# One inference step of a hybrid streaming encoder on one core: the next head's key parts moved beside the scores, memory heads written from PSUM into the projection's operand, open tiles filled chunk by chunk

## Chip, cores and metric

One core of a Trainium2 chip runs the whole step as one program. The metric is the device time of the execution in microseconds (us), the median of several runs; the profile is one execution taken by the hardware profiler.

## What is computed

Two token groups go through a trunk of two layers at once: 1024 new tokens of a stream (the prompt) and 32 tokens of a running stream (the decode group), model width 1024, all in fp32. Layer 0 mixes tokens by causal pooling, layer 1 by differential attention; both attend, with 4 heads of 128 channels, to 256 memory tokens. Cut to what matters here:

```
h = rmsnorm(x, g_attn[l]);  z = h @ w_in[l];  mix, qm = split(z)
m_out = mem_attend(qm, mem_k[l], mem_v[l])                     # 4 memory heads
layer 0:  t_out = pool_mix(mix)                                # 4 groups of 128 channels
layer 1:  k, v = split(rmsnorm(x, g_kv) @ w_kv)                # 4 heads, keys [K1 | K2] of 64 channels each
          for c in (1, 2):  p[c] = softmax(q[c] @ k[c].T / 8 + alibi, chunk-causal)
          t_out = rmsnorm((p[1] - lam * p[2]) @ v, g_subln) * (1 - lam_init)
x = x + concat(t_out, m_out) @ w_out[l]                        # the output projection
x = x + relu(rmsnorm(x, g_ffn[l]) @ w_ff1[l])**2 @ w_ff2[l]
```

Outputs are the final rmsnorm for both groups, the memory keys and values, the new keys and values, and pooling states.

## The kernel before

Activations are kept transposed, 128 channels by tokens: 8 chunks of channels, and the 1056 tokens (1024 + 32) in three groups of 352, the decode tokens at the end of group 2. Each fp32 product is made of three fp32r matmuls: every operand is split into a high part (a cast on ScalarE) and a low part (a subtraction on VectorE or GpSimd; `split`, line 54), and `mm3` (line 47) issues high × high, high × low, low × high. `g_dense` (line 142) makes one output tile of 128 channels by 352 tokens from 8 chunks, 24 matmuls. Weights come by DMA on SP's queue into raw tiles (tag `wraw`, six of them, line 86) and are split ahead of their use (`part`, `weight_split`, `weight`, lines 99 to 132). The operand of the projections is `xh[g]`, `xl[g]` per token group (line 175).

The program is traced in an order written by hand, and a tile scheduler then fixes each engine's order at compile time; each engine runs its own order strictly. The hand-written order is a main stream (a generator of attention work) beside a filler (a generator of projections): `drive` and `step` (lines 476 to 512) advance the main stream by one piece, then at most one piece of the first job in `queue`, then one piece of each job in `side`, and then spend filler matmuls worth `ratio` times the time those pieces say they take. `until(key)` (line 466) yields None until `key` is in `self.done`, which ends the filler's turn; `need` (line 531) runs the filler until something exists.

Layer 1 (`mix1`, line 917): the main stream is `diff_unit` (line 900), four diff-attention heads of four query pairs each (a pair is 256 queries; pair n looks at 256 (n + 1) keys), then `mem_unit` (line 451), four memory heads in two halves of 512 queries. The filler `fill1` (line 938) makes, head by head, the projections of keys, values and queries (`diff_project`, line 679), then the four memory queries (`mem_project`, line 335), then begins the output projection (`open_tiles`, line 953). `diff_project` evicts the keys' three groups into `kst` (line 686, one buffer), the values into `vst` (line 696) and the queries into `qf` (line 705), splits these into `Q` on ScalarE and GpSimd and copies halves of it by DMA. Before the scores of a head, `diff_unit` waits for its projections (`need`), then makes the key parts KS (`diff_keys`, line 729: eight casts of 64 × 256 on ScalarE, lines 736 and 737, and eight subtractions on VectorE, lines 738 and 739; one buffer), rescales the distance table `dtab` (line 906) and goes through the pairs. `diff_scores` (line 767) makes scores (784, 785), adds the table and finds the minimum on VectorE (791), takes the exponential on ScalarE (793), and combines the two maps (764, 765). `diff_values` (808) comes three rounds later: transposes (826), a split of them into `aTh` and `aTl` (55, 56), products with V.

A memory head (`mem_load_kv`, `mem_scores`, `mem_values`, lines 355 to 413): scores, softmax, transposes, split into `aTh`, `aTl`, values in a PSUM tile `po`. Heads 0 to 2 are copied to `mo` on ScalarE (405) and stored to `oscr` in HBM (406); head 3 is split from PSUM into chunk 7 of the operand (413). `mem_sample` (415) does the same for the 32 decode rows of the four heads. `new_x` (948) allocates the operand for the output projection once the last memory query projection is issued. `head` (973) loads a chunk's three token groups from `oscr` into raw tiles and splits them into `xh`, `xl`. `open_tiles` loads chunks 0 to 6 and makes six output tiles from them, two in `dn` banks and four in `sc` banks once the last scores are done; `project` (1013) adds chunk 7 to these six, adds x, and makes the other tiles. The loads of x for this (990, 992) are issued at the start of `tail` (980).

Of the kernel before, what the change touches and what calls it, by code (L numbers as in the profile page):

```python
# [9 lines left out]
F32 = mybir.dt.float32  # L10
F32R = mybir.dt.float32r
# [5 lines left out]
SEQ = 1024  # L17
NS = 32
NT = SEQ + NS
GW = 352  # L20
NG = 3
C = 8
# [8 lines left out]
NRAW = 6  # L31
NWB = 14
WARM = 9
STEPS = 44
LAG = 22
T2_AT, T_AT = 8, 20
ORDER = (2, 0, 1)
YOFF = 896
# [3 lines left out]
class Kern:  # L42
# [188 lines left out]

    def setup(self):
        nc, t, ctx, tc = self.nc, self.t, self.ctx, self.tc
        self.done = set()
        self.pu, self.pend, self.last_exp, self.last_add = {}, [], None, None
        self.wlist, self.wraw, self.wready, self.ahead, self.wstop = self.weights(), [], [], 1, False
        self.base = ctx.enter_context(tc.tile_pool(name="base", bufs=1))
        self.dram = ctx.enter_context(tc.tile_pool(name="dram", bufs=1, space=bass.MemoryType.DRAM))
        self.wpool = ctx.enter_context(tc.tile_pool(name="wpool", bufs=1))
        self.wplace = None  # L240
        self.xpool = ctx.enter_context(tc.tile_pool(name="xpool", bufs=1))
        self.xh, self.xl, self.rs = [None] * NG, [None] * NG, [None] * NG
        b = self.base
        self.gains = b.tile([128, 69], F32, name="gains")
        self.ones = b.tile([128, 128], F32, name="ones")
        nc.vector.memset(self.ones, 1.0)
        self.epsc = b.tile([128, 1], F32, name="epsc")
        nc.vector.memset(self.epsc, EPS)
        self.kscr = [[self.dram.tile([128, 256], F32, name=f"kscr{l}{h}") for h in range(4)] for l in range(2)]
        self.vscr = [[self.dram.tile([128, 2, 128], F32, name=f"vscr{l}{h}") for h in range(4)] for l in range(2)]  # L250
        self.oscr = [[self.dram.tile([128, NT], F32, name=f"oscr{l}{c}") for c in range(8)] for l in range(2)]
        self.xscr = [self.dram.tile([128, C, GW], F32, name=f"xscr{g}") for g in range(NG)]
# [132 lines left out]
    def mem_values(self, l, h, half, p, kv, pr):  # L385
        nc = self.nc
        v = kv[1]
        parts = []
        for a in range(2):
            pt = self.mmtile()  # L390
            for i in range(4):
                b = 256 * i + 128 * a
                nc.tensor.transpose(pt[:, 128 * i:128 * i + 128], pr[:, b:b + 128], self.ident)
            ph = p.tile([128, 512], F32R, tag="aTh", name="aTh", bufs=2)
            pl = p.tile([128, 512], F32R, tag="aTl", name="aTl", bufs=2)
            self.split(ph, pl, pt)
            parts.append((ph, pl))
            yield 0.6
        po = self.mmtile()
        for a in range(2):  # L400
            self.mm3(po, v[:, 0, a], v[:, 1, a], parts[a][0], parts[a][1], a == 0, a == 1)
            yield 0.65
        if h < 3:
            o = p.tile([128, 512], F32, tag="os", name="mo", bufs=2)
            nc.scalar.copy(o, po)
            nc.sync.dma_start(self.oscr[l][4 + h][:, 512 * half:512 * half + 512], o)
            self.done.add(("o", l, h, half))
            return
        for g in range(NG):
            a, b = max(512 * half, g * GW), min(512 * half + 512, (g + 1) * GW)  # L410
            if a < b:
                s = slice(a - g * GW, b - g * GW)
                self.split(self.xh[g][:, C - 1, s], self.xl[g][:, C - 1, s], po[:, a - 512 * half:b - 512 * half])

    def mem_sample(self, l, p, qs):

        nc, t = self.nc, self.t
# [18 lines left out]
        po = self.mmtile()[:, :128]  # L436
        for h in range(4):
            for a in range(2):
                b = 128 * a + NS * h
                nc.tensor.matmul(po[:, NS * h:NS * h + NS], lhsT=vc[:, h, a, :], rhs=aT[:, b:b + NS],  # L440
                                 start=a == 0, stop=a == 1)
        o = p.tile([128, 4, NS], F32, tag="os", name="oss", bufs=2)
        nc.scalar.copy(o.rearrange("p a b -> p (a b)"), po)
        for h in range(3):
            nc.sync.dma_start(self.oscr[l][4 + h][:, SEQ:], o[:, h, :])
        s = slice(GW - NS, GW)
        self.split(self.xh[2][:, C - 1, s], self.xl[2][:, C - 1, s], o[:, 3, :])
        self.done.add(("o", l, "s"))
        yield 0.6

# [228 lines left out]
    def diff_project(self, h, p, out, smp):  # L679
        nc, t = self.nc, self.t  # L680
        W = self.weight()
        kst = self.pd.tile([128, NT], F32, tag="kst", name="kst", bufs=1)
        for g in ORDER if h == 0 else range(NG):
            ps = self.dntile()[:, :GW]
            yield from self.g_dense(ps, W, g)
            nc.vector.tensor_tensor(kst[:, g * GW:(g + 1) * GW], ps, self.rs[g], ALU.mult)
        nc.sync.dma_start(t["kT"][h], kst)

        W = self.weight()
        if h:  # L690
# [2 lines left out]
        for g in range(NG):  # L693
            ps = self.dntile()[:, :GW]
# [6 lines left out]
        for g in range(NG):  # L701
# [22 lines left out]
                        nc.sync.dma_start(qd[o, c], qd[b, c])  # L724
            if g == NG - 1:
                nc.gpsimd.tensor_copy(smp["q"][:, h, :], qf[:, GW - NS:])
        out[h] = {"vst": vst, "kst": kst, "Q": Q}

    def diff_keys(self, h, d, p, smp):
        nc = self.nc  # L730
        kst = d["kst"]
        KS = self.pd.tile([128, 2, SEQ], F32R, tag="ks", name="KS", bufs=1)
        KSf = KS.bitcast(F32)
        for a in range(4):
            s = slice(256 * a, 256 * a + 256)
            nc.scalar.copy(KS[0:64, 0, s], kst[0:64, s])
            nc.scalar.copy(KS[64:128, 1, s], kst[64:128, s])
            nc.vector.tensor_tensor(KS[64:128, 0, s], kst[0:64, s], KSf[0:64, 0, s], ALU.subtract)
            nc.vector.tensor_tensor(KS[0:64, 1, s], kst[64:128, s], KSf[64:128, 1, s], ALU.subtract)
        d["KS"] = KS  # L740
        nc.gpsimd.tensor_copy(smp["k"][:, h, :], kst[:, SEQ:])

    def diff_vals(self, h, d, p, smp):
        nc = self.nc
# [22 lines left out]
    def diff_scores(self, h, pair, p, d, A):  # L767
        nc = self.nc
        Wk = 256 * (pair + 1)
        q = d["Q"][pair]  # L770
        KS = d["KS"]
        for i in (2 * pair, 2 * pair + 1):
            qc = slice((i % 2) * 128, (i % 2) * 128 + 128)
            Wi = max(256, 128 * (i + 1))
# [75 lines left out]
    def diff_sample(self, p, smp):  # L850

        nc, t = self.nc, self.t
        sc = self.sctile()
        kv = self.pd.tile([128, 2, 4, 256], F32, tag="ks", name="kvc", bufs=1)
        kc, vc = kv[:, 0], kv[:, 1].rearrange("p h (a e) -> p h a e", a=2)
        nc.scalar.dma_start(kc, t["ck"])
        nc.scalar.dma_start(vc, t["cv"])
# [42 lines left out]
    def diff_unit(self, p, fill, dd, smp):  # L900
        for h in range(4):
            self.need(fill, dd, h)
            d = dd[h]
            self.diff_keys(h, d, p, smp)
            r = 8.0 * SLOPES[0] if h == 0 else SLOPES[h] / SLOPES[h - 1]
            self.nc.vector.tensor_scalar(self.dtab, self.dtab, r, None, ALU.mult)
            if h:
                yield from self.wait(2)
            self.later(0, self.diff_vals(h, d, p, smp))
            for pair in range(4):  # L910
                A = []
                yield from self.backlog(2)
                yield from self.diff_scores(h, pair, p, d, A)
                self.later(3, self.diff_values(h, pair, p, d, A))
        self.side.append(self.diff_sample(p, smp))

    def mix1(self):
        self.nq, self.nmk = 4, 1
        with self.tc.tile_pool(name="attd", bufs=1, reuse_waits="tile") as self.pd, \
                self.tc.tile_pool(name="att1", bufs=1, reuse_waits="tile") as p:  # L920
            dd, qq = {}, {}
            self.qp = p
            self.claim(self.pd, (("kst", NT, 1), ("vst", NT, 1), ("ks", 2 * SEQ, 1), ("v", 2 * SEQ, 1), ("pA2", 768, 2),
                                 ("std", 8, 4), ("pad", 672, 1)))
            self.claim(p, (("q", 1024, self.nq), ("qf", GW, 2), ("st", 16, 4), ("pA3", 1024, 2), ("aTh", 512, 2),
                           ("aTl", 512, 2), ("mkr", 256, 1), ("mk", 512, 1), ("pad", 128, 1)))
# [26 lines left out]
    def open_tiles(self, l):  # L953

        W = self.W = {}
        self.open = []
        for c in range(C - 1):
            if c > 3:
                for key in (("o", l, c - 4, 0), ("o", l, c - 4, 1), ("o", l, "s")):
                    yield from self.until(key)  # L960
            self.head(l, c)
            if c < 3:
                W[c] = self.weight()
        places = [(0, 0), (0, 1), (0, 2), (1, 0), (1, 1), (1, 2)]
        for n, (g, j) in enumerate(places):
            if n == 2:
                yield from self.until(("m", l, 3, 1))
                X = [t[:, 512 * i:512 * i + 512] for t in (self.sctile(), self.sctile()) for i in range(2)]
            ps = (self.dntile() if n < 2 else X[n - 2])[:, :GW]
            self.open.append((g, j, ps))  # L970
            yield from self.g_dense(ps, W[j], g, range(C - 1))

    def head(self, l, c):

        for g in range(NG):
            o = self.wpool.tile([128, 512], F32, tag="wraw", name="o", bufs=NRAW)[:, :GW]
            self.nc.sync.dma_start(o, self.oscr[l][c][:, g * GW:(g + 1) * GW])
            self.take(o, g, c, pool=())

    def tail(self, l):  # L980
        nc, t = self.nc, self.t
# [658 lines left out]
```

## Time and profile before

| what | us |
|---|---|
| runs: 2127.57, 2129.15, 2131.08; median | 2129.15 |
| the profiled execution's own time | 2129.38 |
| its span, first to last instruction | 2127.6 |
| TensorE (PE) busy | 2093.3 |
| VectorE (DVE) busy | 1686.8 |
| ScalarE (ACT) busy | 1129.7 |
| GpSimd (POOL) busy | 568.3 |

The mean granted TensorE clock is 0.994 of full speed (1 is 2.4 GHz, 0.5 is 1.2 GHz). Times in the rows are us from the start of the span. PE's busy time counts pipelined matmuls with modelled ends. In a row of the trace, "out<-in" names the tile written and those read, and brackets at the end give the idle time of the engine just before and what released it. Layer 0's attention stage runs from about 30 to 225, its feed-forward part to about 960, layer 1's diff attention from about 980 to 1250, its memory heads to 1340, and the rest is layer 1's output projection and feed-forward part.

### The profile page before, as it was taken

What the parts mean: (1) busy time and instruction counts of PE and PEld (TensorE: products, weight loads), DVE (VectorE), ACT (ScalarE), POOL (GpSimd) and SP (SyncE); (2) the same over time, 40 slices, a digit from 0 to 9 for tenths busy, and PEclk for the clock granted to TensorE, in tenths of its full rate; (3) what the DMA queues carried; (4) which work ended last, traced back from release to release, by engine and by line L of the source; (5) the groups of instructions that cost most, each with busy time, mean ns of one, the idle gap of its engine ahead of it and who ended that gap; (6) DMA issues with size and microseconds to landing.
All of it is one profiled execution on the core that took longest, in us unless ns stands there. A gap on an engine that the chain in (4) does not pass through costs nothing. (4 is left out here: it accounts for less than half of the span.)

```text
span 2127.6 us, 35390 instructions
## 1 busy us (share of the span) xinstructions
PE 2093.3 (98%) x13068; PEld 2052.6 (96%) x13068; DVE 1686.8 (79%) x3160; ACT 1129.7 (53%) x2437; POOL 568.3 (27%) x577
## 2 busy tenths in 40 slices
PE   9999999999999999999999999999999999999997
PEld 8999999999999999999998897999999999999997
DVE  8856498888888888867777876489888888888865
ACT  7546364444444444455766766355444444444454
POOL 1021113343334333320111112104333333333323
PEclk9999999999999999999999999999999999999999
DMA  5635321111111111124222114511111111111112
GB/s 194 191 110 184 124 60 56 45 55 45 56 45 55 45 55 45 56 82 154 66 72 74 45 38 134 176 50 50 45 55 45 55 45 55 44 57 45 56 40 82
DMA packets 89997, 159.01 MB, mean 75 GB/s; under 512 B 13280, under 2 KB 32096, under 8 KB 89312
## 3 DMA queue, kind: packets, MB, share of 16 engines
q1 hardware_dynamic: 87952, 151.78, 22.5%
q10 hardware_dynamic: 1872, 4.98, 0.7%
q8 instruction: 102, 1.67, 0.3%
q14 instruction: 71, 0.58, 0.1%
HBM read 127.72 MB, written 24.80 MB: 72 GB/s over the span
## 5 line engine op out<-in xcount | busy, mean ns | idle before, releaser
L50 PE MATMUL dn<-xh,whi 128*128 128x352 f32 x1168 | 384.7, 330 | 6.2 <-ACT xh L55 3.4
L51 PE MATMUL dn<-xl,whi 128*128 128x352 f32 x1168 | 379.7, 325 | 1.8 <-DVE xl L56 1.3
L52 PE MATMUL dn<-xh,wlo 128*128 128x352 f32 x1168 | 379.8, 325 | 0.0
L108 DVE TENSOR_TENSOR wlo<-wraw,whi 128x512 fp32r<-128x512 f32 x344 | 280.8, 820 | 76.9 <-ACT whi L107 76.0
L1334 DVE TENSOR_TENSOR x<-x,mm 128x352 f32<-128x352 f32 x560 | 287.8, 514 | 62.8 <-PE mm L52 62.8
L107 ACT CAST whi<-wraw 128x512 fp32r<-128x512 f32 x344 | 212.2, 620 | 228.7 <-PE dn L51 115.5
L50 PE MATMUL mm<-h2h,whi 128*128 128x352 f32 x832 | 270.4, 325 | 0.0
L52 PE MATMUL mm<-h2h,wlo 128*128 128x352 f32 x832 | 268.0, 322 | 0.0
L51 PE MATMUL mm<-h2l,whi 128*128 128x352 f32 x832 | 266.4, 320 | 0.0
L107 ACT CAST whi<-ws 128x512 fp32r<-128x512 f32 x232 | 143.9, 620 | 220.7 <-PE dn L51 124.2
L1334 DVE TENSOR_TENSOR x<-x,xb 128x352 f32<-128x352 f32 x448 | 223.1, 512 | 26.1 <-PE xb L52 23.4
L50 PEld LDWEIGHTS dn<-xh,whi 128*128 128x128 f32 x1168 | 220.1, 189 | 12.1 <-ACT xh L55 4.6
L51 PEld LDWEIGHTS dn<-xl,whi 128*128 128x128 f32 x1168 | 221.8, 190 | 5.4 <-DVE xl L56 1.5
L52 PEld LDWEIGHTS dn<-xh,wlo 128*128 128x128 f32 x1168 | 221.0, 189 | 0.3
L108 DVE TENSOR_TENSOR wlo<-ws,whi 128x512 fp32r<-128x512 f32 x232 | 179.3, 773 | 3.5 <-ACT whi L107 3.5
L56 POOL TENSOR_TENSOR h2l<-t,h2h 128x352 fp32r<-128x352 f32 x112 | 136.3, 1217 | 171.0 <-ACT h2h L55 171.0
L56 POOL TENSOR_TENSOR h2l<-b,h2h 128x352 fp32r<-128x352 f32 x92 | 116.2, 1277 | 228.8 <-PE mm L52 204.1
L1318 POOL TENSOR_TENSOR t<-b,b 128x352 f32<-128x352 f32 x56 | 64.6, 1153 | 367.6 <-ACT b L1237 367.6
L51 PEld LDWEIGHTS mm<-h2l,whi 128*128 128x128 f32 x832 | 156.3, 188 | 0.4
L50 PEld LDWEIGHTS mm<-h2h,whi 128*128 128x128 f32 x832 | 156.1, 188 | 0.4
L52 PEld LDWEIGHTS mm<-h2h,wlo 128*128 128x128 f32 x832 | 156.2, 188 | 0.0
L52 PE MATMUL dn<-T,wlo 128*128 128x352 f32 x480 | 155.7, 324 | 0.0
(312 smaller groups left out, 5343.6 us busy)
## 6 DMA issues: line engine op xcount, KB each, us to landing
wraw<-in_w_ff SPq DMA_DIRECT2D x256, 256.0 KB, 2.6
wraw<-in_w_out SPq DMA_DIRECT2D x44, 256.0 KB, 3.5
wraw<-in_w_mem SPq DMA_DIRECT2D x32, 256.0 KB, 3.1
wraw<-in_w_in SPq DMA_DIRECT2D x30, 256.0 KB, 3.5
o<-oscr SPq DMA_DIRECT2D x42, 176.0 KB, 3.1
xscr<-x SPq DMA_DIRECT2D x3, 1408.0 KB, 4.8
wraw<-in_w_kv SPq DMA_DIRECT2D x16, 256.0 KB, 3.2
Q<-Q SPq DMA_DIRECT2D x32, 128.0 KB, 2.2
```

What stands on the lines that cost most here:

```text
L50: mm(ps, lhsT=ah, rhs=bh, start=first, stop=False, skip_group_check=more)
L51: mm(ps, lhsT=ah, rhs=bl, start=False, stop=False, skip_group_check=more)
L52: self.last_mm = mm(ps, lhsT=al, rhs=bh, start=False, stop=last, skip_group_check=more)
L56: (lo_eng or self.nc.vector).tensor_tensor(lo, src, hi.bitcast(F32), ALU.subtract)
L107: self.nc.scalar.copy(hi, src)
L108: eng.tensor_tensor(lo, src, hi.bitcast(F32), ALU.subtract)
L1318: self.nc.gpsimd.tensor_tensor(h[out], h[a], h[c], ALU.subtract)
L1334: nc.vector.tensor_tensor(xj, xj, ps, ALU.add)
```

## The change

`diff_keys` becomes a generator. After the second pair's scores of a head (`KEYS_AT = 1`) the next head's is put into `side`; it waits until `diff_project` has issued that head's `kst`, then issues the four slices, one per round. What is left of it runs before that head's scores. KS gets two buffers, and `diff_project` waits, before it makes a head's `kst`, until the parts of the head before are issued. A memory head whose values end their first half after the new operand exists goes from PSUM into it (both halves, and its decode rows), as head 3 did; the others go through `oscr` as before. `head` loads one token group of one chunk, and nothing for a direct head. `open_tiles` loads group 0 of chunks 0 to 2 between the weights, then fills the two `dn` tiles chunk by chunk as chunks are ready, loading group 0 of the next ones; the other groups' loads come after the last scores are issued, one after each chunk of the four `sc` tiles.

```diff
-        self.done = set()
+        self.done, self.direct = set(), set()
@@ mem_values
-        if h < 3:
+        if half == 0 and ("x", l) in self.done:
+            self.direct.add((l, h))
+        if (l, h) not in self.direct:
             o = p.tile([128, 512], F32, tag="os", name="mo", bufs=2)
...
-                self.split(self.xh[g][:, C - 1, s], self.xl[g][:, C - 1, s], po[:, a - 512 * half:b - 512 * half])
+                self.split(self.xh[g][:, 4 + h, s], self.xl[g][:, 4 + h, s], po[:, a - 512 * half:b - 512 * half])
+        self.done.add(("o", l, h, half))
@@ mem_sample
-        for h in range(3):
-            nc.sync.dma_start(self.oscr[l][4 + h][:, SEQ:], o[:, h, :])
-        self.split(self.xh[2][:, C - 1, s], self.xl[2][:, C - 1, s], o[:, 3, :])
+        for h in range(4):
+            if (l, h) in self.direct or h == 3:
+                self.split(self.xh[2][:, 4 + h, s], self.xl[2][:, 4 + h, s], o[:, h, :])
+            else:
+                nc.sync.dma_start(self.oscr[l][4 + h][:, SEQ:], o[:, h, :])
@@ diff_project
+        if h:
+            yield from self.until(("ks", h - 1))
         kst = self.pd.tile([128, NT], F32, tag="kst", name="kst", bufs=1)
...
         nc.sync.dma_start(t["kT"][h], kst)
+        self.kst = kst
+        self.done.add(("k", h))
@@ diff_keys
-        kst = d["kst"]
-        KS = self.pd.tile([128, 2, SEQ], F32R, tag="ks", name="KS", bufs=1)
+        while ("k", h) not in self.done:
+            yield 0.0
+        kst = self.kst
+        KS = self.pd.tile([128, 2, SEQ], F32R, tag="ks", name="KS", bufs=2)
...
             nc.vector.tensor_tensor(KS[0:64, 1, s], kst[64:128, s], KSf[64:128, 1, s], ALU.subtract)
-        d["KS"] = KS
+            yield 0.0
+        self.KS[h] = KS
         nc.gpsimd.tensor_copy(smp["k"][:, h, :], kst[:, SEQ:])
+        self.done.add(("ks", h))
@@ diff_unit
-            self.diff_keys(h, d, p, smp)
+            if h == 0:
+                keys = self.diff_keys(0, smp)
+            for _ in keys:
+                pass
...
                 self.later(3, self.diff_values(h, pair, p, d, A))
+                if pair == KEYS_AT and h < 3:
+                    keys = self.diff_keys(h + 1, smp)
+                    self.side.append(keys)
@@ open_tiles
         W = self.W = {}
-        self.open = []
-        for c in range(C - 1):
-            if c > 3:
-                for key in (("o", l, c - 4, 0), ("o", l, c - 4, 1), ("o", l, "s")):
-                    yield from self.until(key)
-            self.head(l, c)
-            if c < 3:
-                W[c] = self.weight()
+        todo = [(g, c) for g in range(NG) for c in range(C - 1)]
+        def ready(c):
+            return c < 4 or {("o", l, c - 4, 0), ("o", l, c - 4, 1), ("o", l, "s")} <= self.done
+        def heads(n, groups=NG):
+            for x in [x for x in todo if x[0] < groups and ready(x[1])][:n]:
+                self.head(l, x[1], x[0])
+                todo.remove(x)
+        for j in range(3):
+            heads(1, 1)
+            W[j] = self.weight()
         places = [(0, 0), (0, 1), (0, 2), (1, 0), (1, 1), (1, 2)]
-        for n, (g, j) in enumerate(places):
-            if n == 2:
-                yield from self.until(("m", l, 3, 1))
-                X = [t[:, 512 * i:512 * i + 512] for t in (self.sctile(), self.sctile()) for i in range(2)]
-            ps = (self.dntile() if n < 2 else X[n - 2])[:, :GW]
-            self.open.append((g, j, ps))
-            yield from self.g_dense(ps, W[j], g, range(C - 1))
+        banks = [self.dntile()[:, :GW] for _ in range(2)]
+        for c in range(C - 1):
+            while not ready(c):
+                yield None
+            while (0, c) in todo:
+                heads(1, 1)
+            for n in range(2):
+                yield from self.g_dense(banks[n], W[n], 0, [c])
+                if n:
+                    heads(1, 1)
+        self.open = [places[n] + (banks[n],) for n in range(2)]
+        yield from self.until(("m", l, 3, 1))
+        X = [t[:, 512 * i:512 * i + GW] for t in (self.sctile(), self.sctile()) for i in range(2)]
+        for n, (g, j) in enumerate(places[2:]):
+            self.open.append((g, j, X[n]))
+            for c in range(C - 1):
+                while (g, c) in todo:
+                    heads(1)
+                yield from self.g_dense(X[n], W[j], g, [c])
+                heads(1)
+        heads(len(todo))
-    def head(self, l, c):
-        for g in range(NG):
-            o = self.wpool.tile([128, 512], F32, tag="wraw", name="o", bufs=NRAW)[:, :GW]
-            self.nc.sync.dma_start(o, self.oscr[l][c][:, g * GW:(g + 1) * GW])
-            self.take(o, g, c, pool=())
+    def head(self, l, c, g):
+        if (l, c - 4) in self.direct:
+            return
+        o = self.wpool.tile([128, 512], F32, tag="wraw", name="o", bufs=NRAW)[:, :GW]
+        self.nc.sync.dma_start(o, self.oscr[l][c][:, g * GW:(g + 1) * GW])
+        self.take(o, g, c, pool=())
```

The decode group's cached keys and values (`kvc`, line 854) share the two buffers of KS.

## Rows read from the trace of the kernel before

**Rows 1.** The page, part 1: busy time, share of the span and instructions.

```profile
PE 2093.3 (98%) x13068; PEld 2052.6 (96%) x13068; DVE 1686.8 (79%) x3160; ACT 1129.7 (53%) x2437; POOL 568.3 (27%) x577
```

**Rows 2.** PE's waits over the whole span: total us, times, longest us.

```profile
PE mm L50 <- ACT aTh L55: 6.8, 3, 2.5
...
PE mm L393 <- ACT mo L405: 0.2, 1, 0.2
```

**Rows 3.** Stretches: length, busy time (count) by engine, granted clock, DMA share, GB/s.

```profile
1070.00:1080.00 10.00, 7.48 (x41) 6.90 (x40) 3.60 (x9) 3.66 (x10) 2.42 (x5) 0.83 0.39 106
1130.00:1145.00 15.00, 12.04 (x72) 11.53 (x71) 9.51 (x20) 7.34 (x21) 3.77 (x6) 0.89 0.35 91
1195.00:1205.00 10.00, 7.35 (x41) 6.59 (x40) 8.75 (x24) 6.84 (x22) 3.19 (x5) 0.83 0.23 52
1305.00:1330.00 25.00, 20.63 (x111) 15.90 (x110) 19.33 (x40) 16.45 (x46) 4.71 (x7) 0.86 0.56 185
1340.00:1345.00 5.00, 4.21 (x26) 3.97 (x26) 3.10 (x8) 2.75 (x7) 0.00 (x0) 1.00 0.93 285
1320.00:1325.00 5.00, 3.41 (x20) 2.69 (x19) 5.00 (x11) 3.36 (x12) 0.00 (x0) 1.00 0.28 90
```

**Rows 4.** Timeline of PE at the second border (start, us, what).

```profile
1130.12 0.28 PE L50 MATMUL mm<-aTh,V 128*128 128x256 f32 x1
...
1135.23 0.39 PE L50 MATMUL mm<-aTh,V 128*128 128x256 f32 x1 [1.86 <-ACT aTh L55]
```

**Rows 5.** Timeline of ScalarE at the second border.

```profile
1133.20 1.36 ACT L55 CAST Q<-qf 64x64 fp32r<-64x64 f32 x4 [0.72 <-DVE qf L705]
1134.59 0.59 ACT L55 CAST aTh<-mm 128x512 fp32r<-128x512 f32 x1
```

**Rows 6.** Timeline of VectorE at the second border.

```profile
1132.65 0.52 DVE L705 TENSOR_TENSOR qf<-dn,rs 128x352 f32<-128x352 f32 x1
```

**Rows 7.** Groups by line, VectorE, 1120 to 1140; line 739's durations (min/median/max).

```profile
L739 DVE TENSOR_TENSOR KS<-kst,KS 64x256 fp32r<-64x256 f32 x4 | 2.3, 572 | 0.1
...
L738 DVE TENSOR_TENSOR KS<-kst,KS 64x256 fp32r<-64x256 f32 x4 | 2.0, 496 | 0.1
...
L739 DVE TENSOR_TENSOR KS<-kst,KS x16: 420/422/870, 998.3 to 1197.5; 64x256 fp32r<-64x256 f32 x16
```

**Rows 8.** Timeline of ScalarE at the first border.

```profile
1070.52 1.36 ACT L55 CAST Q<-qf 64x64 fp32r<-64x64 f32 x4 [0.40 <-DVE qf L705]
...
1072.22 0.56 ACT L55 CAST aTh<-mm 128x512 fp32r<-128x512 f32 x1
```

**Rows 9.** Timelines: last third of kst (VectorE, heads 1, 2), first key cast (ScalarE).

```profile
1041.00 0.50 DVE L686 TENSOR_TENSOR kst<-dn,rs 128x352 f32<-128x352 f32 x1
...
1089.79 0.52 DVE L686 TENSOR_TENSOR kst<-dn,rs 128x352 f32<-128x352 f32 x1
...
1051.70 0.40 ACT L736 CAST KS<-kst 64x256 fp32r<-64x256 f32 x1
```

**Rows 10.** Stretches in the middle of the head between borders one and two.

```profile
1090.00:1110.00 20.00, 19.99 (x129) 18.54 (x128) 16.64 (x48) 15.19 (x39) 0.91 (x3) 1.00 0.15 54
1110.00:1122.00 12.00, 12.00 (x77) 11.46 (x76) 10.78 (x28) 10.51 (x23) 0.20 (x1) 1.00 0.26 85
```

**Rows 11.** Groups by line, ScalarE, 1260 to 1350.

```profile
L55 ACT CAST xh<-o 128x352 fp32r<-128x352 f32 x21 | 9.8, 489 | 6.6 <-DMA o<-oscr 6.5
```

**Rows 12.** Timeline of PE in the memory heads.

```profile
1312.56 0.95 PE L50 MATMUL dn<-xh,whi 128*128 128x352 f32 x2 [2.66 <-ACT xh L55]
```

**Rows 13.** Timeline of ScalarE in the memory heads.

```profile
1311.50 0.62 ACT L107 CAST whi<-wraw 128x512 fp32r<-128x512 f32 x1 [1.07 <-DMA wraw<-in_w_out]
```

**Rows 14.** Timeline of SP's queue at the end of the memory heads.

```profile
1339.59 0.36 SPq L990 DMA_DIRECT2D x<-xscr  x1
```

**Rows 15.** Timeline of VectorE in the output projection.

```profile
1357.01 1.90 DVE L108 TENSOR_TENSOR wlo<-wraw,whi 128x512 fp32r<-128x512 f32 x3
```

**Rows 16.** The tile oscr: us from issue to landing, all its transfers.

```profile
DMA to landing us min/median/max: 1.4/2.5/5.8
```

More of the change, by code (lines that the diff above doesn't have):

```diff
@@ L35 @@
 LAG = 22
+KEYS_AT = 1
 T2_AT, T_AT = 8, 20
@@ L726, in diff_project, with diff_keys @@
                 nc.gpsimd.tensor_copy(smp["q"][:, h, :], qf[:, GW - NS:])
-        out[h] = {"vst": vst, "kst": kst, "Q": Q}
-    def diff_keys(self, h, d, p, smp):
+        out[h] = {"vst": vst, "Q": Q}
+    def diff_keys(self, h, smp):
         nc = self.nc
-        kst = d["kst"]
-        KS = self.pd.tile([128, 2, SEQ], F32R, tag="ks", name="KS", bufs=1)
+        while ("k", h) not in self.done:
+            yield 0.0
+        kst = self.kst
+        KS = self.pd.tile([128, 2, SEQ], F32R, tag="ks", name="KS", bufs=2)
         KSf = KS.bitcast(F32)
@@ L770, in diff_scores @@
         q = d["Q"][pair]
-        KS = d["KS"]
+        KS = self.KS[h]
         for i in (2 * pair, 2 * pair + 1):
@@ L853, in diff_sample @@
         sc = self.sctile()
-        kv = self.pd.tile([128, 2, 4, 256], F32, tag="ks", name="kvc", bufs=1)
+        kv = self.pd.tile([128, 2, 4, 256], F32, tag="ks", name="kvc", bufs=2)
         kc, vc = kv[:, 0], kv[:, 1].rearrange("p h (a e) -> p h a e", a=2)
@@ L920, in mix1 @@
                 self.tc.tile_pool(name="att1", bufs=1, reuse_waits="tile") as p:
-            dd, qq = {}, {}
+            dd, qq, self.KS = {}, {}, {}
             self.qp = p
-            self.claim(self.pd, (("kst", NT, 1), ("vst", NT, 1), ("ks", 2 * SEQ, 1), ("v", 2 * SEQ, 1), ("pA2", 768, 2),
+            self.claim(self.pd, (("kst", NT, 1), ("vst", NT, 1), ("ks", 2 * SEQ, 2), ("v", 2 * SEQ, 1), ("pA2", 768, 2),
                                  ("std", 8, 4), ("pad", 672, 1)))
@@ L955, in open_tiles @@
         W = self.W = {}
-        self.open = []
-        for c in range(C - 1):
-            if c > 3:
-                for key in (("o", l, c - 4, 0), ("o", l, c - 4, 1), ("o", l, "s")):
-                    yield from self.until(key)
-            self.head(l, c)
-            if c < 3:
-                W[c] = self.weight()
-        places = [(0, 0), (0, 1), (0, 2), (1, 0), (1, 1), (1, 2)]
-        for n, (g, j) in enumerate(places):
-            if n == 2:
-                yield from self.until(("m", l, 3, 1))
-                X = [t[:, 512 * i:512 * i + 512] for t in (self.sctile(), self.sctile()) for i in range(2)]
-            ps = (self.dntile() if n < 2 else X[n - 2])[:, :GW]
-            self.open.append((g, j, ps))
-            yield from self.g_dense(ps, W[j], g, range(C - 1))
@@ new lines, in open_tiles @@
+        for j in range(3):
+            heads(1, 1)
+            W[j] = self.weight()
+        places = [(0, 0), (0, 1), (0, 2), (1, 0), (1, 1), (1, 2)]
+        banks = [self.dntile()[:, :GW] for _ in range(2)]
+        for c in range(C - 1):
+            while not ready(c):
[6 more added lines that the diff above has]
+                    heads(1, 1)
```

## The prediction, made before the result was known

> **What bounds the kernel now.** I read the page first, then PE's waits, then tables by stage, then single stretches in order of time. TensorE is busy 98% of the span [rows 1]; the change adds and removes no matmul, so all it can give back is time in which PE stands still or runs at its lower clock. PE does nothing in 34 us, and its own waits name the largest cause [rows 2]: 6.8 us in three waits for `aTh` from ScalarE, 2.5 at most. Cut by stage, the gaps lie in two places that the change touches [rows 3]. At the three borders between diff-attention heads PE stands still for 2.52, 2.96 and 2.65 us (length less busy time), 8.1 in sum. Behind each the mean granted clock of the stretch is 0.83, 0.89 and 0.83: a share at 1.2 instead of 2.4 GHz, which costs (1 − clock) × length = 1.7, 1.65 and 1.7 us more. So a border costs about 4.4 us, the three 13.2. In the end of the memory heads 1305 to 1330 loses 4.37 us of standing still and 3.5 of clock, 1340 to 1345 another 0.79: 8.7 in sum. In layer 0 the only wait of PE in this code is one of 0.2 us, for `mo` [rows 2]: nothing to win there.
>
> **Why PE stops at a border.** Take the second one. PE starts the values at 1135.23, after 1.86 us of waiting for `aTh` [rows 4]. `aTh` stood on ScalarE at 1134.59, behind four casts of Q that began at 1133.20 after waiting 0.72 for `qf` [rows 5]. `qf` (L705) came at 1132.65 [rows 6], although PE began what follows the last of its matmuls at 1130.12 [rows 4], since VectorE was busy without a gap with the key parts of the next head (L738, L739) and one L765. In that stretch the eight key subtractions took 4.3 us (0.50 and 0.57 each), where one alone takes 0.42 [rows 7]; ScalarE makes eight casts of 0.40 beside them [rows 9]. The third border repeats this pattern 63 us on. At the first, `aTh` is behind the Q casts as well: they begin at 1070.52, it at 1072.22 [rows 8].
>
> **Part 1, the keys beside the scores.** Per head 8 ScalarE casts and 8 VectorE subtractions (8 × 0.40 = 3.2 and 8 × 0.42 = 3.4 us) leave the border and may run once `kst` is whole and the second pair's scores are issued. No matmul and no DMA moves. The second buffer removes the wait of the new parts on the last score matmuls of the head before. The new wait (`kst` of a head on the parts of the head before) has the K projection queued behind it in the filler, but those parts are out two projections earlier. The last third of `kst` of head 1 is evicted at 1041.0 and the first key cast follows at 1051.7: 10 us of room. For head 2 `kst` is whole at 1089.8 [rows 9], over 30 us ahead of the border; head 3 repeats it.
> Second and third border: with 4.3 us off VectorE, `qf` can follow its matmuls at 1130.3 instead of 1132.65, the Q casts at about 1130.9 (key casts are gone from ScalarE too), `aTh` at 1132.3 and `aTl` by 1133.6, where PE arrives at 1133.4, 1.86 ahead of 1135.23. I leave 0.5 us at each. A stall so short leaves the clock alone: the stretch from 1320 to 1325 stands still for 1.6 us at a clock of 1.00 [rows 3]. Gain 2.96 + 1.65 + 2.65 + 1.7 − 1.0 = 8.0. First border: without 3.4 us of keys the `wlo` parts and with them the loads and `whi` casts of the next weight come some 3 us earlier; then `aTh` either goes ahead of the last Q casts (no stall) or stays behind them (1.36 + 0.56 = 1.9 us and what lies between, as now). Half of 4.2: 2.1.
> What it costs at its new place: VectorE has 3.36 us free of 20 in 1090 to 1110 [rows 10], for 3.4 us of work. PE has no gap there, covered by the projection of the next head; if that cover were late, each head could lose up to the 3.4 us. Bounds 0 to 10.2; I take 0.5 per head, 1.5, near the lower end, since in 1110 to 1122 VectorE has only 1.2 of 12 us free and PE loses nothing [rows 10]. Part 1: −8.0 − 2.1 + 1.5 = −8.6; bounds −13.2 and, with the borders unchanged, +10.2.
>
> **Part 2, the memory heads and the open tiles.** A head that goes from PSUM into the operand saves two copies to `mo`, two stores, three loads and the three casts from `o` of 0.49 [rows 11], and pays four shorter casts instead. Head 2 of layer 1 should become direct, as its values are issued after the new operand exists. Neither is on the path by itself. What counts is the order of loads. Before, they go chunk by chunk for all three groups between the output weights, and all share six buffers. PE stands 2.66 us until 1312.56 for an `xh` [rows 12]; just ahead ScalarE was held until 1311.50 by a weight that had not landed [rows 13], with the key cast of the last memory head behind it. With one load in place of three between weights, four loads fewer stand ahead of that point; at 0.49 of ScalarE each this is some 2 us. The stall of 2.66 shrinks to about 0.6, of the 3.5 us of clock I count half (whether the rest is short enough is open), of the later 1.6 half, and the 0.79 goes, as the open tiles read groups 0 and 1 alone and no longer come after loads that wait for the decode rows. That is 2.1 + 1.75 + 0.8 + 0.8 = 5.4.
> What is late next: the tail's x loads are issued from 1339.59 [rows 14] and its weights behind them, and the next output weight's `wlo` begins at 1357.01 [rows 15], by its place in the timeline some 2 us ahead of the matmuls that need it. A PE that comes earlier by more waits there, except for what x itself comes earlier. So I take 3.5 of the 5.4; bounds −8.7 and, if the loads come late, +5 (below). A direct head holds its PSUM bank through ScalarE and VectorE, as head 3 does now with no PE wait beside it: nothing, as another bank serves the transposes.
> Here row and rule part. The slowest transfer from or to `oscr` took 5.8 us to land, where the median is 2.5 [rows 16]. The Trainium skill (DMA: Bandwidth & Descriptors, section "Issuing engines are not separate DMA queues") says that all DMAs run on the same 16 engines and interleave, whichever engine started them. By that rule every load of groups 1 and 2 that slips behind the x loads would pay this, which is the third rival. The trace shows it for single loads, and PE did not wait for them.
>
> **Sum.** −8.6 − 3.5 = −12.1 on the profiled execution's own 2129.38 us (span 2127.6); that execution stands 0.23 above the median of the three runs, 2129.15. So 2117.2, say **2117.5 us**.
>
> **Rivals.**
> (a) The borders keep half: `aTh` stays behind the Q casts in ScalarE's order whatever VectorE does. For it: at the first border that order alone makes the stall. Against: at the other two `qf` was 2.3 us late by VectorE. Then 13.2 / 2 − 1.5 = 5.1 from the heads and half of the tail's gain: 2122.5 (2119 to 2127).
> (b) Slower. The keys run in the middle of the head, the score evictions (L791) behind them are late, and PE, whose order is fixed, meets a score or `aTh` that is not there: two stalls a head of one border's size. Two stalls of 2.4 with one drop of clock (1.7) cost 6.5, 19.5 for three heads, against 13.2 + 3.5 won: 2129.4 + 2.8 = 2132. It decides from the point where VectorE's 3.4 us free in 20 are not where the keys fall due. For it: 83% busy, and 90% just after [rows 10]. Against: PE loses nothing at 90%.
> (c) The tail gives nothing or loses: loads of groups 1 and 2 land behind x, PE waits up to 3.3 us (5.8 − 2.5) once plus 1.7 of clock: the 3.5 becomes +5, with part 1 in full: 2126. With the tail merely unchanged: 2121.
> (d) It doesn't do what it says: the keys' turn comes only at the border, because `kst` is issued late. For it only head 1 (1041.0). Then the tail's gain alone is left: 2126.
>
> **Chances.** Forecast 0.55, (a) 0.2, (b) 0.08, (c) 0.12, (d) 0.05. About 0.2% (4.3 us) can be told from no change. Faster by more: 0.55, and most of (a) and of (c), 0.79; slower by more: (b) below its full price and a worse (c) included, 0.09; within: 0.12. The range leaves out (b) above and all stalls gone (−22) below: 2109 to 2127. The forecast's own range is 2110 to 2122.
>
> **What would show it.** Right: no wait of PE for `aTh` above 1 us, a clock of 1.00 at each border, key casts within some 15 us of `kst`, 36 `o<-oscr` loads or fewer instead of 42, no `xh` wait above 1 us in the memory heads, and the span shorter by the stalls gone. Wrong: key subtractions still within 5 us of the border; new PE waits for L791's or L55's output in the middle of a head; PE waiting for `wlo` or x in the output projection after the open tiles.

## The result and the profile after

The changed kernel takes 2106.39 us (median of 4 runs, 2102.99 to 2107.51) beside 2128.36 for the kernel before: a ratio of 0.9894, with a 95% interval of 0.9877 to 0.9911. That is 22.0 us faster. The forecast was 12.1 us faster, and the time lies 2.6 us below the range of 2109 to 2127. The direction and the two places were right; the size was not.

The page of the changed kernel, part 1, answers to [rows 1]:

```profile
PE 2081.7 (99%) x13068; PEld 2045.3 (97%) x13068; DVE 1683.4 (80%) x3164; ACT 1125.7 (53%) x2437; POOL 568.0 (27%) x577
```

The span is 2105.2 us, 22.4 shorter. With the same 13068 matmuls PE stands still for 2105.2 − 2081.7 = 23.5 us, where it was 34.3 (10.8 less), and is busy for 11.6 us less, as more of them run at the full clock (mean granted clock 0.997, before 0.994). PE's waits (us in total, times, longest) answer to [rows 2]: the longest of the stage, and what is left of `aTh`, which stood at 6.8 in three:

```profile
PE sc L51 <- ACT mk L56: 1.7, 1, 1.7
...
PE mm L51 <- ACT aTh L56: 0.2, 1, 0.2
```

The stretches around the three borders and the end of the memory heads (length, busy time by engine, granted clock, DMA share, GB/s) answer to [rows 3]:

```profile
1060.00:1075.00 15.00, 14.66 (x99) 14.33 (x98) 7.27 (x18) 8.67 (x25) 6.95 (x13) 1.00 0.52 142
1120.00:1135.00 15.00, 14.62 (x99) 14.37 (x98) 11.05 (x25) 10.22 (x26) 7.05 (x12) 1.00 0.44 114
1180.00:1195.00 15.00, 15.00 (x104) 14.67 (x103) 13.45 (x36) 13.21 (x36) 8.04 (x14) 1.00 0.61 172
1285.00:1310.00 25.00, 22.73 (x148) 20.02 (x147) 19.30 (x42) 17.41 (x52) 5.45 (x9) 1.00 0.53 156
1310.00:1330.00 20.00, 20.00 (x129) 18.46 (x128) 10.56 (x23) 9.60 (x27) 1.13 (x2) 1.00 0.34 110
1330.00:1350.00 20.00, 19.86 (x125) 19.55 (x124) 10.45 (x18) 7.75 (x15) 5.05 (x5) 1.00 0.83 312
```

At the borders PE stands still for 0.34, 0.38 and 0.00 us, at a clock of 1.00. Of the 13.2 us counted there 0.7 are left: 12.5 won. For the end, here is the kernel before over the same three stretches of time:

```profile
1285.00:1310.00 25.00, 24.90 (x152) 22.80 (x151) 16.51 (x35) 15.33 (x44) 6.00 (x10) 0.93 0.45 139
1310.00:1330.00 20.00, 15.73 (x81) 11.63 (x82) 14.53 (x29) 13.02 (x34) 3.08 (x5) 0.83 0.49 163
1330.00:1350.00 20.00, 19.21 (x120) 17.74 (x120) 7.96 (x18) 7.81 (x22) 1.07 (x2) 1.00 0.60 206
```

Standing still is 0.10 + 4.27 + 0.79 = 5.2, and the clock costs 0.07 × 25 + 0.17 × 20 = 5.2: 10.3 us. After, it is 2.27 + 0 + 0.14 = 2.4 with the clock at 1.00. But the 0.07 × 25 = 1.75 of clock before 1310 were not won. They lie at 1288 to 1291, right behind the decode group's diff attention, and as the same work now runs some 10 to 15 us earlier, the changed kernel has that drop just ahead of these stretches, again without standing still:

```profile
1270.00:1285.00 15.00, 15.00 (x85) 13.41 (x84) 9.25 (x19) 7.93 (x25) 3.81 (x5) 0.89 0.17 56
```

It costs 0.11 × 15 = 1.65 there. So the end won 10.3 − 2.4 − 1.65 = 6.2 us by these sums, and borders and end make 18.7 of the 22.4.

There is a second way to count. Both traces have 13068 matmuls, so the starts of the n-th of each can be set side by side. In the changed kernel the 6200th (before: at 996) starts 0.7 us earlier, the 7800th (at 1256, behind the diff heads) 13.8, the 9000th (at 1458) and all later ones 22.1. So the diff heads gave 13.1 and what follows them 8.3. What these have above 12.5 and 6.2 is in neither the standing still nor the clock of the rows, and stays open; the 0.7 ahead of them is no more than traces differ there (e7 below, which changes nothing ahead of that point, shows 1.5).

### The profile page after: what moved, and what is told of

The parts are those of the page before. It is cut to its first block, busy times and chain, and to the rows that moved or that the text cites. A ratio compares the mean times of both kernels' runs of the same rounds, so it can differ in the third digit from the quotient of the medians.

```text
span 2105.2 us, 35352 instructions
## 1 busy us (share of the span) xinstructions
PE 2081.7 (99%) x13068; PEld 2045.3 (97%) x13068; DVE 1683.4 (80%) x3164; ACT 1125.7 (53%) x2437; POOL 568.0 (27%) x577
```

## The experiments

Each kernel was timed beside the kernel before on the same chip; across chips the ratio is what compares.

| kernel | median us | before beside it | ratio, 95% interval |
|---|---|---|---|
| e1 keys alone | 2115.67 | 2129.86 | 0.9934, 0.9921 to 0.9948 |
| e2 memory heads and open tiles alone | 2121.47 | 2129.86 | 0.9967, 0.9954 to 0.9979 |
| e3 changed, old open tiles | 2122.32 | 2129.86 | 0.9968, 0.9957 to 0.9978 |
| e4 changed, no new direct head | 2104.89 | 2129.86 | 0.9889, 0.9875 to 0.9902 |
| e5 changed, subtractions at the border | 2108.51 | 2128.20 | 0.9906, 0.9893 to 0.9920 |
| e6 changed, keys after the last scores | 2109.43 | 2128.20 | 0.9911, 0.9898 to 0.9925 |
| e7 before, two KS buffers | 2115.73 | 2128.57 | 0.9938, 0.9926 to 0.9950 |
| e8 changed, loads by chunk | 2121.22 | 2128.20 | 0.9967, 0.9957 to 0.9978 |
| e9 changed, tile after tile | 2107.00 | 2128.20 | 0.9900, 0.9886 to 0.9913 |
| e10 changed, one KS buffer | 2120.87 | 2128.57 | 0.9967, 0.9956 to 0.9978 |
| e11 two buffers and loads by group | 2104.31 | 2128.57 | 0.9889, 0.9876 to 0.9902 |
| e12 as e8, group 2 last | 2106.60 | 2127.89 | 0.9900, 0.9884 to 0.9915 |

### The two halves, one at a time

e1 holds the hunks of `diff_project`, `diff_keys` and `diff_unit` and the buffers; e2 those of `mem_values`, `mem_sample`, `open_tiles` and `head`.

> Keys part alone (memory heads and open tiles as before). The change as a whole gave 22.0 us. Theory A (each part gives back its own stalls in full): the trace of after loses 12.0 us less than before by the end of the diff heads, so this kernel gains 11 to 13 us, about 2116.4, its three borders show no PE wait for aTh over 0.4 us, and its memory heads still lose some 9 us in 1290 to 1335. Theory B (the sizes of the prediction hold for the keys, the rest of the gain is an interplay): it gains 8 to 9 us, 2119.5 to 2120, and PE waits at a border or in the middle of a head for the difference.

> Memory heads and open tiles of the change, the key parts at the border as before. Theory A: what after wins behind the diff heads (about 9.4 us of the 21.9 in the two traces) is this part's own, so 2118 to 2120, with the three borders losing 13 to 15 us as before and the tail losing some 3 us in place of 11. Theory B: the part gives the 3.5 us of the prediction, about 2125, and the rest came because the diff heads were over earlier.

e1 gained 14.2 us, e2 8.4; the sum, 22.6, is about the whole (22.0). PE's wait with the largest sum in 1000 to 1250, first of e1, then of e2:

```profile
PE mm L52 <- DVE aTl L57: 0.7, 2, 0.4
```

```profile
PE mm L50 <- ACT aTh L55: 6.7, 3, 2.5
```

The halves add up, and each gave back its own stalls about in full: theory A, with both times within 1.5 us of what it expected. The forecast's 8.6 and 3.5 were both too small.

### What in the tail did it

e3 puts back the old `open_tiles` and a `head` that loads three groups; e4 changes one line:

```diff
-        if half == 0 and ("x", l) in self.done:
+        if half == 0 and h == 3:
```

> The changed kernel with the open tiles of before (seven chunks of three groups loaded between the weights, tile after tile), direct heads and key parts as in the change. Theory L (the order of the loads in the six raw tiles is what stopped PE in the tail): 5 to 8 us slower than the changed kernel, 2111.5 to 2114.5, with ScalarE held by a wraw load and PE by an xh in 1285 to 1320 again. Theory D (the direct heads did it, by three loads, three casts and two copies fewer per head): within 2 us of the changed kernel, 2105 to 2108.

> The changed kernel with only the last memory head direct, as before; open tiles by chunk and key parts as in the change. Theory L: the order of the loads is kept, so at most 2 us slower than the changed kernel, 2106 to 2108.5. Theory D: the gain of the tail goes, 4 to 7 us slower, 2110 to 2113, with PE waiting for the xh of head 2's chunk once its loads come back from oscr.

Without the new direct heads nothing is lost: e4's interval lies on that of the changed kernel. Without the new open tiles 14 to 16 us are lost, twice what theory L expected. That is more than e2 had gained; with the old open tiles, direct heads cost 2122.32 − 2115.67 = 6.7 us against e1. PE's waits for the exponentials `pr` of a memory head, in e3 and in e1:

```profile
PE sc L51 <- ACT pr L551: 4.2, 3, 2.2
```

```profile
PE sc L51 <- ACT pr L546: 2.1, 1, 2.1
```

Why direct heads make these longer under the old order was not tried. That the cost goes with the order of the loads, e8 and e12 below show: both have the direct heads.

The open tiles changed in two ways, in the order of loads and in the order of matmuls. e8 keeps the matmuls by chunk and loads a chunk's three groups together (`heads(3)` in all three places where `heads(1, 1)` stood); e9 keeps the loads by group and makes the two tiles one after the other:

```diff
 e8
-        todo = [(g, c) for g in range(NG) for c in range(C - 1)]
+        todo = [(g, c) for c in range(C - 1) for g in range(NG)]
...
-            heads(1, 1)
+            heads(3)
 e9
-            for n in range(2):
-                yield from self.g_dense(banks[n], W[n], 0, [c])
-                if n:
-                    heads(1, 1)
+        for n in range(2):
+            yield from self.g_dense(banks[n], W[n], 0, range(C - 1))
```

> The changed kernel whose open tiles load a chunk's three groups at once and in the order of the chunks, as before, while the first two tiles are still filled chunk by chunk. Theory L (order of loads: a group 1 or 2 tile that waits for decode rows or heads holds up the raw tiles behind it): 5 to 15 us slower than the changed kernel, 2111 to 2121. Theory F (matmuls to fill with: by chunk, the first tiles' matmuls of chunks 0 to 3 can be issued beside the memory heads, where before none could until head 2 was out): within 3 us of the changed kernel, 2105 to 2109.

> The changed kernel with the loads by group as in the change, but the first two open tiles made one after the other once chunk 6 is issued, so that no matmul of theirs can be issued beside memory heads 0 to 2. Theory L: within 3 us of the changed kernel, 2105 to 2109. Theory F: 5 to 15 us slower, 2111 to 2121, with PE standing still for ScalarE's exponentials or mk between 1290 and 1330.

Theory F falls: e9 is as fast as the changed kernel. e8 loses some 15 us, like e3, and so 7 more than the tail had won. Stretches of e8, then of e9:

```profile
1290.00:1310.00 20.00, 16.36 (x93) 13.94 (x92) 16.02 (x32) 14.01 (x40) 5.89 (x8) 0.91 0.81 255
1310.00:1350.00 40.00, 35.10 (x199) 30.75 (x200) 18.84 (x44) 17.30 (x51) 4.38 (x7) 0.96 0.49 177
```

```profile
1285.00:1310.00 25.00, 24.78 (x157) 21.27 (x156) 21.47 (x50) 20.29 (x64) 5.72 (x9) 1.00 0.50 153
1310.00:1350.00 40.00, 39.86 (x249) 38.42 (x249) 17.39 (x34) 14.02 (x30) 7.14 (x8) 1.00 0.59 211
```

Which loads hold up the others, SP's queue of e8 shows (start, us, what):

```profile
1286.86 1.74 SPq L911 DMA_DIRECT2D oscr<-ofs  x4
...
1289.12 0.43 SPq L1018 DMA_DIRECT2D o<-oscr  x1
1289.59 0.94 SPq L88 DMA_DIRECT2D wraw<-in_w_out  x2
...
1296.84 0.89 SPq L88 DMA_DIRECT2D wraw<-in_w_out  x2
...
1301.15 0.94 SPq L88 DMA_DIRECT2D wraw<-in_w_out  x2
```

The load at 1289.12 is the first one of group 2, for chunk 0. It reads the decode rows, which `ofs` stores in four transfers from 1286.86. Six output weights, issued behind it into the same six raw tiles, come at 1289.59, 1296.84 and 1301.15, two each. The kernel before has the same pattern, 9 us later:

```profile
1295.56 1.75 SPq L896 DMA_DIRECT2D oscr<-ofs  x4
...
1297.83 0.43 SPq L977 DMA_DIRECT2D o<-oscr  x1
1298.30 0.92 SPq L87 DMA_DIRECT2D wraw<-in_w_out  x2
```

In the changed kernel nothing of group 2 stands ahead of them, and the six are out between 1177 and 1255:

```profile
1171.51 0.36 SPq L1018 DMA_DIRECT2D o<-oscr  x1
1177.07 0.33 SPq L88 DMA_DIRECT2D wraw<-in_w_out  x1
...
1255.19 0.33 SPq L88 DMA_DIRECT2D wraw<-in_w_out  x1
```

e12 tests just this. It is e8 with group 2 put last (in the same three places):

```diff
-            heads(3)
+            heads(2, 2)
```

> The run with loads by chunk (2121.2) with one thing put back: group 2 of every chunk, which holds the decode rows, is loaded last, as in the change; groups 0 and 1 still come chunk by chunk between the output weights. Theory G (the first load of group 2 waits until the diff heads' decode rows are stored at about 1286, and the output weights behind it in the six raw tiles wait with it until 1289): nearly all comes back, 2104 to 2110, with the six output weights issued by 1270. Theory C (it is the count of loads and their casts of 0.49 us ahead of the weights): one third fewer gives back a third, 2114 to 2118.

All of it came back, although two loads in place of one still stand ahead of each weight: theory G, not the count. Whether the weights had waited for a raw tile or only for their place behind that load in SP's order, the runs do not part. SP's queue of e12, with the first and the last of the six weights, both ahead of `ofs`, and the first load behind it:

```profile
1188.08 2.86 SPq L88 DMA_DIRECT2D wraw<-in_w_out  x2
...
1269.24 1.52 SPq L88 DMA_DIRECT2D wraw<-in_w_out  x2
...
1283.86 1.75 SPq L911 DMA_DIRECT2D oscr<-ofs  x4
...
1289.35 0.32 SPq L1018 DMA_DIRECT2D o<-oscr  x1
```

### What in the keys did it

e5 leaves the casts beside the scores and makes the subtractions in a loop of their own once the head's turn has come; e6 has `KEYS_AT = 3`.

> The changed kernel with its eight key casts (ScalarE) left beside the scores and its eight key subtractions (VectorE) put back to the border. Theory V (what made aTh late was VectorE: qf behind the subtractions, then the Q casts behind qf): most of the 14 us that the keys gave alone is lost again, 2114 to 2120, with PE waits for aTh of 1 us or more at the second and third border. Theory S (ScalarE's order, its 3.2 us of key casts ahead of the Q casts and aTh, made it late): at most 4 us slower than the changed kernel, up to 2110.

> The changed kernel with the key parts of the next head begun after the fourth pair's scores in place of the second's. Theory R (the parts need room: their place in the order written by hand decides, and late in the head they meet qf and the values): 3 to 10 us slower than the changed kernel, 2109.5 to 2116, with key subtractions within 5 us of a border and PE waits for aTh there. Theory N (any place ahead of the border does, since the casts only wait for kst, which is whole 25 us ahead): the changed kernel's time within 2 us.

Both missed what they were made for. VectorE's timeline of e5 around head 1 has the first third of `kst`, and the first and the last of the eight subtractions, which the written order has only at the border:

```profile
1024.67 0.53 DVE L694 TENSOR_TENSOR kst<-dn,rs 128x352 f32<-128x352 f32 x1 [0.18 <-PE dn L53]
...
1025.95 0.42 DVE L756 TENSOR_TENSOR KS<-kst,KS 64x256 fp32r<-64x256 f32 x1
...
1050.87 0.42 DVE L757 TENSOR_TENSOR KS<-kst,KS 64x256 fp32r<-64x256 f32 x1
```

The scheduler puts the parts where their inputs and their buffer are free, whatever the written order. The changed kernel has nearly the same picture: the first subtraction comes while two thirds of `kst` are still to be made, the last 9 us after it is whole.

```profile
1023.25 0.53 DVE L694 TENSOR_TENSOR kst<-dn,rs 128x352 f32<-128x352 f32 x1 [0.18 <-PE dn L53]
...
1024.53 0.42 DVE L751 TENSOR_TENSOR KS<-kst,KS 64x256 fp32r<-64x256 f32 x1
...
1048.63 0.42 DVE L752 TENSOR_TENSOR KS<-kst,KS 64x256 fp32r<-64x256 f32 x1
```

So e5 decides nothing between V and S, and e6 speaks for N, with up to some 4 us open, as the intervals of e5 and e6 touch that of the changed kernel. The hint was in the kernel before: its key casts of heads 1 to 3 start at 1051.70, 1124.40 and 1187.85 ([rows 9] has the first), and the last matmul that reads the KS before ends 1.4, 3.1 and 3.1 us ahead of them; for the second, at 1121.26:

```profile
1120.87 0.39 PE L785 MATMUL sc<-KS,Q 128*128 128x512 f32 x1
```

e7 tests the buffer alone, on the kernel before, and e10 takes it out of e6:

```diff
 e7
-        KS = self.pd.tile([128, 2, SEQ], F32R, tag="ks", name="KS", bufs=1)
+        KS = self.pd.tile([128, 2, SEQ], F32R, tag="ks", name="KS", bufs=2)
 e10
-KEYS_AT = 1
+KEYS_AT = 3
...
-        KS = self.pd.tile([128, 2, SEQ], F32R, tag="ks", name="KS", bufs=2)
+        KS = self.pd.tile([128, 2, SEQ], F32R, tag="ks", name="KS", bufs=1)
```

> The kernel before with one number changed: KS (and the cached keys that share its tag) get two buffers; the key parts keep their place in the order written by hand, at the border. Theory B (the single buffer held them: in the trace of before the first key cast comes 2.5 to 4.2 us after the last scores of the head before begin, and in the two runs in which the parts were put late in the written order they still ran in the middle of the head): most of what the keys alone gave, 11 to 15 us, so 2114 to 2118, with key subtractions 20 us or more ahead of the border. Theory P (the place in the written order did it): no change, 2126 to 2130, key subtractions within 5 us of the border.

> The changed kernel with one KS buffer; the parts therefore begin, by the written order, after the fourth pair's scores (the run with that place and two buffers took 2109.4). Theory B: 10 to 15 us slower than that run, 2119 to 2125, with the border waits of before (aTh, 1.5 us and more each). Theory P: 2108 to 2112.

e7 gained 12.8 us with the order written by hand untouched, as much as e1 within the intervals. The last of its key subtractions starts at 1152.0, where it stood at 1197.5 [rows 7] (ns of one, min, median and max, then first and last start):

```profile
L739 DVE TENSOR_TENSOR KS<-kst,KS x16: 420/421/422, 997.0 to 1152.0; 64x256 fp32r<-64x256 f32 x16
```

e10 lost some 11 us against e6, and the border waits were back (in the stretches the clock is the third number from the end):

```profile
PE mm L51 <- ACT aTh L56: 7.7, 3, 2.8
```

```profile
1065.00:1080.00 15.00, 12.25 (x66) 11.65 (x65) 5.10 (x12) 6.63 (x19) 4.27 (x9) 0.77 0.39 104
1125.00:1140.00 15.00, 12.61 (x74) 11.77 (x73) 12.63 (x28) 10.47 (x27) 6.24 (x10) 0.89 0.41 104
1190.00:1205.00 15.00, 11.90 (x73) 11.31 (x73) 13.57 (x34) 11.20 (x32) 5.58 (x9) 0.89 0.32 83
```

Theory B holds in both directions. The Trainium skill (Trainium Kernel Development and Optimization, section "Best Practices") advises two buffers so that DMA runs beside compute; in e7 the second buffer gave 12.8 us for a tile that engines alone write and read at these borders.

### The small version

e11 is the kernel before with two KS buffers and the open tiles of the change (loads by group, the first two tiles chunk by chunk); the keys stay at the border in the written order, and one head is direct.

> The kernel before with two things only: two KS buffers and the open tiles of the change (loads by group); key parts at the border in the written order, only the last memory head direct. If theory B and theory L are the whole of the change, it does as well as the changed kernel: 2103 to 2109. If the place of the keys or the direct heads are worth something of their own, it is 3 us or more slower, 2110 to 2116.

It matches the changed kernel (0.9889 and 0.9894, the intervals overlap); no kernel is clearly faster than that. The place of the keys and the direct heads are worth nothing that these runs can tell.

## Why the prediction was wrong, step by step

Two steps failed. In Part 1 three costs were deducted, 1.0 for the second and third border, 2.1 for the first and 1.5 for the keys' new place; they measured 0.4, 0.3 and about 0.7. In Part 2 the stall was put down to a count of loads and given 3.5; one load that could not start had made it, and 8.3 came. Beside these, the gain of Part 1 was credited to the wrong half of its edit.

- **The bound and the places** were right: ahead of layer 1's attention 0.7 us changed and behind the 9000th matmul nothing, and no matmul went.
- **"Why PE stops at a border"** named the right chain, keys on VectorE ahead of `qf`, Q casts, `aTh`. The cause behind it was misread. "May run once `kst` is whole and the second pair's scores are issued": the parts run third by third, and what had kept them at the border was the single buffer, not their place (e7, e10). The text named that wait, and credited the move. Its signs of being right could not tell the two apart: no wait for `aTh` above 1 us, a clock of 1.00 at each border, key casts soon behind `kst` and 36 loads all came.
- **"I leave 0.5 us at each"**: 0.38 and 0.00 were left at the second and third border. **"Half of 4.2: 2.1"** at the first: the whole came, less 0.34. `aTh` is still behind the Q casts there, but these begin at 1067.13 in place of 1070.52 [rows 8], and only some 1.2 us of that is PE's own earlier arrival:

```profile
1067.13 1.37 ACT L56 CAST Q<-qf 64x64 fp32r<-64x64 f32 x4
1068.53 0.59 ACT L56 CAST aTh<-mm 128x512 fp32r<-128x512 f32 x1
```

- **"I take 0.5 per head, 1.5"** for the keys' new place: in 45 us of the middle of two heads PE stands still for 0.30 and 0.18 at a clock of 1.00, where it did for 0.01 and 0.00 in 45 us between the same borders before. So some 0.25 per head. The kernel before, then the changed one:

```profile
1080.00:1125.00 45.00, 44.99 (x292) 42.85 (x291) 36.56 (x98) 33.74 (x84) 2.85 (x7) 1.00 0.17 58
1145.00:1190.00 45.00, 45.00 (x291) 42.87 (x290) 38.04 (x101) 34.82 (x87) 3.35 (x8) 1.00 0.18 60
```

```profile
1075.00:1120.00 45.00, 44.70 (x291) 42.72 (x290) 38.12 (x103) 35.34 (x89) 1.98 (x6) 1.00 0.16 58
1135.00:1180.00 45.00, 44.82 (x291) 42.71 (x290) 37.91 (x101) 34.50 (x87) 1.53 (x5) 1.00 0.18 58
```

With that the keys come to 12.5 − 0.7 = 11.8 by the stretches, 13.1 by the count of matmuls (e1: 14.2, e7: 12.8, by medians), where 8.6 was taken.

- **Part 2** failed in its reading, not just in size. "With one load in place of three between weights, four loads fewer stand ahead" put the delay down to a count of loads at 0.49 us each. e8's queue and e12 show that it was one load that could not start: chunk 0's group 2, waiting for decode rows. The text saw such a wait for the last loads only and gave it 0.79. With the weights out by 1255, the 2.66 us wait for `xh` [rows 12] and the held ScalarE [rows 13] are gone.
- **"So I take 3.5 of the 5.4"**, for x and `wlo` being late next: they weren't. x is issued from 1323.78 in place of 1339.59 [rows 14], and PE stands still for 0.14 us in 1330 to 1350. The tail gave 6.2 by the stretches, 8.3 by the count of matmuls, 8.4 in e2.
- **The direct heads**, "Neither is on the path by itself": right with the new order of loads (e4), not with the old one, where they cost 6.7 (e3 against e1).
- **The rivals.** (a): no border kept half. (b): no stall in the middle of a head came near 2.4 us. (c): the slowest transfer from or to `oscr` takes 4.8 us to land, where it was 5.8 [rows 16] (min, median, max):

```profile
DMA to landing us min/median/max: 1.4/2.6/4.8
```

By the rule of the Trainium skill (DMA: Bandwidth & Descriptors, section "Issuing engines are not separate DMA queues") these loads share 16 engines with x; that sharing does not show in PE's waits here. (d): the first key subtraction of head 1 comes 1.3 us after the first third of `kst`.
- **The range.** "all stalls gone (−22)" was worked out and left out below. Each term had been cut for a cost that then did not come, and all the cuts pointed the same way. Taken in full, 13.2 + 8.7 = 21.9 lies close to the 22.0 that came, in part by luck: 0.7 us are left at the borders and 0.5 in the middle of two heads, the end has 2.4 of standing still, and the sums by stretches explain 18.7.

## What to carry to other kernels

Where a scheduler places instructions by their inputs and buffers, look for the buffer that holds a late instruction back before moving it in the program: its start just behind the last reader of the old contents gives it away, and one more buffer may be the whole change. In a ring of tiles that is filled in order, look for the one load that cannot start, not for the number of loads; put what depends on late results last. And if a stall's cause goes away, count the whole stall with the drop of the clock right behind it, and subtract only for a successor that a row shows.

## What was not expected of the hardware

The wait of 1.7 us for `mk` (in the waits above, at 1299.40) left the granted clock at 1.00: 1285 to 1310 holds 2.27 us of standing still in all and no lower clock. In e10 stretches of 15 us with 2.75, 2.39 and 3.10 us of it show 0.77, 0.89 and 0.89. In these rows the shorter stall cost no clock at all, so a stall cut down to that size gave back more than the time cut from it.

The clock also fell where PE does not stand still by the rows. In both kernels it is at 0.50 right behind the decode group's diff attention, 24 matmuls of 32 columns each, and the change took nothing from that. The first of them before, then a stretch before and one after:

```profile
1284.83 0.53 PE L887 MATMUL mm<-dsT,kvc 128*128 128x32 f32 x4
```

```profile
1288.00:1290.00 2.00, 2.00 (x8) 1.64 (x8) 0.00 (x0) 0.78 (x3) 0.00 (x0) 0.50 0.00 0
1278.00:1280.00 2.00, 2.00 (x10) 1.93 (x9) 1.12 (x2) 1.02 (x3) 0.00 (x0) 0.50 0.12 42
```

PE counts as busy there, with modelled ends. The key subtractions, 0.42 to 0.87 us each at the old border [rows 7], all take 0.42 where they run now.
